# A gated linear unit in three passes of split operands, two gate tiles interleaved by halves of x, and the own-key part of attention on GpSimd

## The chip, the cores and the metric

The kernel runs on one core of a Trainium2 chip. The metric is the device time of one execution in microseconds (us), as the median of several runs.

## What is computed

One decoder layer over 1024 tokens of width 1024, in float32. The input is normalised and projected; half of the channels go through a diagonal state-space branch (S5), half through attention with a sliding window of 128 keys; both are gated, projected out, normalised, added to the input, and a gated embedding is added. What matters here, cut from the reference:

```python
# state-space branch: y is the output of the scan, 512 channels
g = jax.nn.gelu(y)
out = g * jax.nn.sigmoid(g @ w_glu + b_glu)          # the gated linear unit
ssm_out = out * jax.nn.silu(z_ssm)                   # z_ssm: 512 columns of the projection
# attention: each block of 128 queries sees the previous and its own block of keys
e = jnp.exp(scores - m)
probs = e / (jnp.sum(e, axis=-1, keepdims=True) + jnp.exp(sink - m))
out = jnp.einsum('bnkgqs,bnskd->bnqkgd', probs, vb)
mixed = jnp.concatenate([ssm_out, attn_out], axis=-1) @ w_out
```

## The kernel before

Everything lies transposed: channels on the 128 partitions, tokens along the free axis. A tensor of 512 channels has four tiles of 128 x 1024; a product with 1024 input channels runs over eight k-tiles of 128. TensorE accumulates in PSUM banks of 128 x 512, so a 1024-token result takes a pair of banks, one for each half of the tokens.

Most products are made with split operands. A float32 tile t is split into hi (a copy rounded to the type F32R, by ScalarE) and lo (t minus hi, by VectorE; `split_to`, L95). `products` (L119) then runs three F32R matmuls for each k-tile and half: weights hi times activations hi, weights hi times activations lo, weights lo times activations hi (L126, L128, L130). `load_split` (L108) loads weights through a staging tile w_st (two buffers) and splits them into w_hi and w_lo (four buffers each, of 128 x 4 x 128). The gated linear unit is the exception: there, y and w_glu are plain float32 and each k-tile takes one float32 matmul (L929).

After the state-space scan and most of the projection, a stage begins in which attention and other work share TensorE. The order of TensorE's work is written out by hand there. The other work is cut into "pieces", numbered n, which a table (`pieces`, filled by `at(n, f)`, L857) maps to functions. A time step t runs the attention steps that are due and then, except in every eighth step, the next piece. The order on the other engines is planned from the order of the program and priorities; attention steps have a higher priority (`AHEAD`).

The pieces, in their order:

- SsmGate (L866): the last two tiles (m = 2 and 3) of the state-space gate z. Each tile is a product over the eight k-tiles of x, one k-tile a piece: tile 2 has pieces 0 to 7, tile 3 has 8 to 15. Then come three steps: two scalings on VectorE out of PSUM, a tanh on ScalarE, and a product on VectorE, whose result goes to DRAM (z_dr). x lies in four big tiles: hi and lo of the first four k-tiles, hi and lo of the last four.
- `load_y` (L945), at piece 12: the output y of the scan comes back from DRAM (y_dr) in eight loads of 256 KB into a big tile y_all.
- Glu (L903): for each half hf of the tokens and each tile m, two pieces (16 to 31 in all), with two float32 matmuls each (L929). Three pieces before the first of them w_glu[m] is loaded (eight loads in all), one piece before it the gate's half tile z. Behind them come a tanh on ScalarE out of PSUM, two VectorE operations ((th + 1) y, and that times z / 2; L936, L937) and a split into m_hi and m_lo.
- OutHalf (L964): the product of m_hi and m_lo with the upper half of w_out, from piece 32 on; the first tile reads the tiles m = 0 to 2 at pieces 32 to 34 and m = 3 at piece 38.

Attention goes in 16 units, two to a block of 128 queries (even units: half 0, PSUM bank "w"; odd units: half 1, bank "y"). The steps of a unit: scores (TensorE; on GpSimd a copy of the sinks, L781), maxima (VectorE, out of PSUM, L796 and L804), exponents (ScalarE, L811), normalised (VectorE in even units, ScalarE in odd ones, L821 and L819), transposed (four TensorE transposes into a bank, then a ScalarE copy of it to a tile p, L826 and L828), parted (L830), values (L837) and gated (VectorE, L849). The 128 keys of the window lie in one row of 128, where a key of the previous block and one of the own block share a column. So values takes p times the previous block's v, plus the own-key part of p (p_own) times the difference of the two blocks' v (v_step). p_own is p times a triangular mask of ones (own_t), made by VectorE out of the same PSUM bank that ScalarE copies (L834). The values step of an even unit and the following odd unit come at the same time step: six steps after the transposes of the even one, two after those of the odd one.

Big tiles (128 x 4096 values, tag t16) have seven buffers. GpSimd also issues the query DMAs (L760, L761), four to a block.

Of the kernel before, what the change touches and what calls it, by code (L numbers as in the profile page):

```python
# [20 lines left out]
P = 128  # L21
D = 1024
T = 1024
KT = D // P
# [29 lines left out]
def layer_kernel(  # L54
# [6 lines left out]
    with ExitStack() as top:  # L61
# [685 lines left out]
        own_t = flat[:, 160:288]  # L747
        Q.memset(own_t, 1.0)
        Q.affine_select(out=own_t, in_=own_t, compare_op=ALU.is_ge, fill=0.0, base=0, pattern=[[1, P]], channel_multiplier=-1)

# [16 lines left out]
        class Unit:  # L767
# [62 lines left out]
            def parted(self):  # L830

                if self.b:
                    self.own = t2([P, 4, P], F32, "p_own", "qt")
                    V.tensor_tensor(out=self.own, in0=self.pt.rearrange("p (m q) -> p m q", m=4),  # L834
                                    in1=own_t.unsqueeze(1).broadcast_to([P, 4, P]), op=ALU.mult)
# [30 lines left out]
        class SsmGate:  # L866


            def __init__(self, m, n):
                self.m = m  # L870
                at(n - 3, self.load)
                for k in range(KT):
                    at(n + k, self.multiply, k)
                for i, f in enumerate((self.scale, self.tanh, self.store)):
                    at(n + KT + i, f)
# [27 lines left out]
        class Glu:  # L903


            def __init__(self, hf, m, n):
                self.hf, self.m = hf, m
                at(n - 3, self.load)
                at(n - 1, self.load_gates)
                for k in range(2):  # L910
                    at(n + k, self.multiply, k)
# [3 lines left out]
            def load(self):  # L915
                self.w = t2([P, 4, P], F32, "w_glu", "w_hi")
                with behind((self.hf, self.m) > (0, 1) and glu_in["last"]):
                    nc.sync.dma_start(out=self.w, in_=w_glu[self.m])

            def load_gates(self):  # L920
                self.zt = t4([P, 2, HALF], F32, "z_th")
                with behind(glu_in["last"]):
                    nc.sync.dma_start(out=self.zt[:, 0].rearrange("p (i c) -> p i c", i=HC), in_=z_dr[self.m][:, HC * self.hf : HC * self.hf + HC, :])

            def multiply(self, n):
                if n == 0:
                    self.ps = bank("mm")
                for k in (2 * n, 2 * n + 1):
                    PE.matmul(self.ps, lhsT=self.w[:, k, :], rhs=glu_in["y"][:, self.hf, k, :], start=k == 0, stop=k == 3)  # L929
# [4 lines left out]
            def gate(self):  # L934
                z, th = self.zt[:, 0], self.zt[:, 1]
                V.scalar_tensor_tensor(out=th, in0=th, scalar=1.0, in1=glu_in["y"][:, self.hf, self.m, :], op0=ALU.add, op1=ALU.mult)  # L936
                V.scalar_tensor_tensor(out=th, in0=th, scalar=0.5, in1=z, op0=ALU.mult, op1=ALU.mult)  # L937
# [5 lines left out]
        glu_in, glu_out = {}, []  # L943

        def load_y():  # L945
            y = glu_in["y"] = t16([P, 2, 4, HALF], F32, "y_all")
# [266 lines left out]
```

## Time and profile before

| | |
|---|---|
| median of 3 runs | 509.57 us (509.54 to 511.63) |
| the profiled execution | 510.56 us, its span 508.9 us |
| TensorE busy | 500.0 us, 98% of the span |
| VectorE busy | 372.6 us, 73% |
| ScalarE busy | 212.3 us, 42% |
| GpSimd busy | 35.0 us, 7% |

PE is TensorE, PEld its weight loads, DVE VectorE, ACT ScalarE, POOL GpSimd and SPq the queue that issues most DMAs. An instruction is told as line, engine, operation, output <- inputs, shapes. Matmuls are pipelined and the durations in the profile overlap, so the cost of one in a row of equal ones is read from start to start; the same holds for VectorE. A float32 matmul stands in the trace as two records. In brackets stands how long the engine had been idle before an instruction and what ended that.

### The profile page before, as it was taken

To read this page: it belongs to the slowest core of one execution; us is meant where nothing else is said; L and a number is where in the kernel's file an instruction comes from. 1 tells how busy PE (TensorE), PEld (TensorE's weight loads), DVE (VectorE), ACT (ScalarE), POOL (GpSimd) and SP (SyncE) were. 2 spreads that over 40 slices of the span, in tenths; PEclk is the share of its full clock that TensorE was granted. 3 is DMA by queue.
4 is the path that set the end of the run, shared out by engine and by line. 5 is a ranking of instruction groups with operands and counts; after the bars stand their busy time and mean duration, and the time that the engine had idled before them with its cause. 6 is when DMAs were issued, how large, how long until landed. Compare 5 with 4: busy or idle time off the path is not lost.

```text
span 508.9 us, 7268 instructions
## 1 busy us (share of the span) xinstructions
PE 500.0 (98%) x2445; PEld 403.2 (79%) x2445; DVE 372.6 (73%) x873; ACT 212.3 (42%) x450; POOL 35.0 (7%) x71
## 2 busy tenths in 40 slices
PE   7999999999999999999999999999999999999996
PEld 5788888888888888887555777877888888888886
DVE  3869999999999998557888766535565589564332
ACT  5777031322122232357566665556533362232311
POOL 1000000000000005231201320000000000000000
PEclk9999999999999999999999999999999999999999
DMA  7981624445555444564944521010212334134112
GB/s 257 394 261 60 201 84 134 124 120 149 140 133 133 119 139 108 155 178 155 301 165 146 175 63 32 22 41 1 103 63 82 124 120 130 42 124 146 62 43 83
DMA packets 54389, 65.05 MB, mean 128 GB/s; under 512 B 18384, under 2 KB 33232, under 8 KB 54352
## 3 DMA queue, kind: packets, MB, share of 16 engines
q1 hardware_dynamic: 50960, 58.09, 36.4%
q0 software_dynamic: 1536, 4.20, 3.1%
q10 hardware_dynamic: 1856, 2.31, 1.9%
q8 instruction: 19, 0.31, 0.3%
q14 instruction: 18, 0.15, 0.1%
HBM read 44.12 MB, written 11.01 MB: 108 GB/s over the span
## 4 chain that ended last, share of the span: by engine, by line
PE 88%; DVE 7%; DMA 2%; ACT 1%; issue 1%; SPq 0%; ACTq 0%
PE ps_mm L126 20%; PE ps_mm L128 19%; PE ps_mm L130 19%; PE ps_mm L929 6%; PE ps_tab L126 4%; PE ps_tab L128 4%; PE ps_tab L130 4%; PE ps_w L844 2%; PE ps_tab L788 1%; PE ps_y L635 1%; PE ps_tab L787 1%; PE ps_y L637 1%; PE ps_tab L546 1%; PE ps_y L844 1%; DMA x_st<-in_xT 1%; PE ps_w L559 1%
## 5 line engine op out<-in xcount | busy, mean ns | idle before, releaser
L96 ACT ACTIVATE w_hi<-w_st 128x512 fp32r<-128x512 f32 (+1 forms) x63 | 39.1, 620 | 120.1 <-PE ps_mm L128 70.6
L126 PE MATMUL ps_mm<-x_hi,w_hi 128*128 128x512 f32 x272 | 87.2, 396 | 1.8 <-ACT x_hi L194 1.4
L128 PE MATMUL ps_mm<-x_lo,w_hi 128*128 128x512 f32 x272 | 86.3, 395 | 0.6 <-DVE x_lo L195 0.6
L130 PE MATMUL ps_mm<-x_hi,w_lo 128*128 128x512 f32 x272 | 86.3, 393 | 0.0
L97 DVE TENSOR_TENSOR w_lo<-w_st,w_hi 128x512 fp32r<-128x512 f32 (+1 forms) x63 | 42.4, 673 | 27.0 <-ACT w_hi L96 24.3
L126 PEld LDWEIGHTS ps_mm<-x_hi,w_hi 128*128 128x128 f32 x272 | 50.1, 188 | 12.2 <-ACT x_hi L194 1.8
L128 PEld LDWEIGHTS ps_mm<-x_lo,w_hi 128*128 128x128 f32 x272 | 50.5, 188 | 11.2 <-DVE x_lo L195 1.4
L130 PEld LDWEIGHTS ps_mm<-x_hi,w_lo 128*128 128x128 f32 x272 | 50.9, 188 | 10.4
L811 ACT ACTIVATE sc<-sc,mx 128x129 f32<-128x129 f32 x64 | 25.1, 393 | 21.8 <-DVE mx L804 21.8
L128 PE MATMUL ps_mm<-h_lo,w_hi 128*128 128x512 f32 (+1 forms) x96 | 30.8, 380 | 0.0
L126 PE MATMUL ps_mm<-h_hi,w_hi 128*128 128x512 f32 (+1 forms) x96 | 30.8, 380 | 0.0
L130 PE MATMUL ps_mm<-h_hi,w_lo 128*128 128x512 f32 (+1 forms) x96 | 30.7, 380 | 0.0
L929 PE MATMUL ps_mm<-y_all,w_glu 128*128 128x512 f32 x64 | 29.7, 597 | 0.0
L1110 DVE SCALAR_TENSOR_TENSOR o_t<-o_t,pls 128x512 f32<-128x512 f32 (+1 forms) x17 | 10.8, 658 | 19.5 <-ACT o_t L1109 19.5
L126 PE MATMUL ps_mm<-m_hi,w_hi 128*128 128x512 f32 x64 | 21.2, 412 | 0.0
L128 PEld LDWEIGHTS ps_mm<-h_lo,w_hi 128*128 128x128 f32 x96 | 18.1, 188 | 3.5
L130 PEld LDWEIGHTS ps_mm<-h_hi,w_lo 128*128 128x128 f32 x96 | 18.0, 188 | 3.5
L126 PEld LDWEIGHTS ps_mm<-h_hi,w_hi 128*128 128x128 f32 x96 | 18.0, 188 | 3.4
L929 PEld LDWEIGHTS ps_mm<-y_all,w_glu 128*128 128x128 f32 x64 | 11.3, 189 | 11.3 <-issue 10.4
L128 PE MATMUL ps_mm<-m_lo,w_hi 128*128 128x512 f32 x64 | 19.9, 392 | 0.0
L130 PE MATMUL ps_mm<-m_hi,w_lo 128*128 128x512 f32 x64 | 19.9, 392 | 0.0
L781 POOL COPY sc<-sink 128x4 f32<-128x4 f32 x16 | 13.7, 855 | 75.4 <-PE ps_y L826 44.8
(279 smaller groups left out, 1021.6 us busy)
## 6 DMA issues: line engine op xcount, KB each, us to landing
w_st<-in_w_in SPq DMA_DIRECT2D x30, 256.0 KB
w_st<-in_w_out SPq DMA_DIRECT2D x16, 256.0 KB
w_st<-in_w_gate SPq DMA_DIRECT2D x16, 256.0 KB
x<-in_xS SPq DMA_DIRECT2D x8, 512.0 KB
out_T<-o_t SPq DMA_DIRECT2D x15, 256.0 KB
x_sq<-in_xT SPq DMA_DIRECT2D x4, 512.0 KB
x_st<-in_x SPq DMA_DIRECT2D x4, 512.0 KB
x_sq<-in_x SPq DMA_DIRECT2D x4, 512.0 KB
```

Of the source, the lines that this page charges most:

```text
L96: S.activation(hi, t, AF.Copy)
L97: V.tensor_tensor(out=lo, in0=t, in1=hi.bitcast(F32), op=ALU.subtract)
L126: yield PE.matmul(o, lhsT=wh, rhs=ah(ka, h), start=f, stop=False)
L128: yield PE.matmul(o, lhsT=wh, rhs=al(ka, h), start=False, stop=False)
L130: yield PE.matmul(o, lhsT=wl, rhs=ah(ka, h), start=False, stop=l)
L546: PE.matmul(ps[:, j, 0 : PC + P], lhsT=mt[:, g * P : (g + 1) * P], rhs=flat[:, 288 * j + 16 * odd : 288 * j + 16 * odd + PC + P], start=Tr ...
L559: PE.matmul(ps[:, g * NC : (g + 1) * NC], lhsT=m[:, g * P : (g + 1) * P], rhs=U[:, g, :], start=True, stop=True)
L781: Q.tensor_copy(out=self.sc.rearrange("p (a b) s -> p a b s", a=2)[:, :, :, P], in_=sink.rearrange("p (a b) -> p a b", a=2)[:, :, self.ms])
L811: S.activation(self.sc[:, m, :], self.sc[:, m, :], AF.Exp, bias=self.mx[:, m : m + 1], scale=-1.0, accum_out=self.sm[:, m : m + 1])
L844: PE.matmul(pv[64 * kv : 64 * kv + 64], lhsT=v[:, cols], rhs=p[:, 2 * kv : 2 * kv + 2, :], start=n == 0, stop=n == len(parts) - 1)
L929: PE.matmul(self.ps, lhsT=self.w[:, k, :], rhs=glu_in["y"][:, self.hf, k, :], start=k == 0, stop=k == 3)
L1110: V.scalar_tensor_tensor(out=t, in0=t, scalar=1.0, in1=pls[2 * m + h][:, a : a + n], op0=ALU.add, op1=ALU.mult)
```

## The change

Four things. The two gate tiles are interleaved: pieces 0 to 3 are tile 2 over the first four k-tiles of x, 4 to 7 tile 3 over the same, 8 to 11 tile 2 over the last four, 12 to 15 tile 3. y is loaded at piece 8, first half of the tokens first, and split into y_hi (ScalarE) and the low part in place (VectorE), tile by tile, at pieces 11 to 14 (first half) and 16 to 22 (second half). The gated linear unit runs `product` on split operands; w_glu is loaded and split once for both halves, its low part made by GpSimd. The gate loads both z and y by half tiles, and a VectorE operation z y / 2 (`weigh`) stands before the tanh, one operation behind it. The own-key part is selected on GpSimd from the copy p in SBUF.

```diff
-        own_t = flat[:, 160:288]
-        Q.memset(own_t, 1.0)
-        Q.affine_select(out=own_t, in_=own_t, compare_op=ALU.is_ge, fill=0.0, base=0, pattern=[[1, P]], channel_multiplier=-1)
...
                 if self.b:
                     self.own = t2([P, 4, P], F32, "p_own", "qt")
-                    V.tensor_tensor(out=self.own, in0=self.pt.rearrange("p (m q) -> p m q", m=4),
-                                    in1=own_t.unsqueeze(1).broadcast_to([P, 4, P]), op=ALU.mult)
+
+                    Q.affine_select(out=self.own, in_=self.p, compare_op=ALU.is_ge, fill=0.0, base=0,
+                                    pattern=[[0, 4], [1, P]], channel_multiplier=-1)
...
-            def __init__(self, m, n):
+            def __init__(self, m, ns):
                 self.m = m
-                at(n - 3, self.load)
-                for k in range(KT):
-                    at(n + k, self.multiply, k)
+                at(ns[0] - 3, self.load)
+                for k, n in enumerate(ns):
+                    at(n, self.multiply, k)
                 for i, f in enumerate((self.scale, self.tanh, self.store)):
-                    at(n + KT + i, f)
+                    at(ns[-1] + 1 + i, f)
...
-                at(n - 3, self.load)
+                if hf == 0:
+                    at(n - 3, self.load)
                 at(n - 1, self.load_gates)
+                at(n + 1, self.weigh)
...
             def load(self):
-                self.w = t2([P, 4, P], F32, "w_glu", "w_hi")
-                with behind((self.hf, self.m) > (0, 1) and glu_in["last"]):
-                    nc.sync.dma_start(out=self.w, in_=w_glu[self.m])
+                hi, lo = t2([P, 4, P], F32R, "g_hi", "w_hi"), t2([P, 4, P], F32R, "g_lo", "w_lo")
+                st = t2([P, 4, P], F32, "w_st", "w_st")
+                with behind(self.m > 1 and glu_in["last"]):
+                    nc.sync.dma_start(out=st, in_=w_glu[self.m])
+                S.activation(hi, st, AF.Copy)
+                Q.tensor_tensor(out=lo, in0=st, in1=hi.bitcast(F32), op=ALU.subtract)
+                glu_w.append([(hi, lo)])
...
-                    nc.sync.dma_start(out=self.zt[:, 0].rearrange("p (i c) -> p i c", i=HC), in_=z_dr[self.m][:, HC * self.hf : HC * self.hf + HC, :])
+                    for i, t in enumerate((z_dr, y_dr)):
+                        nc.sync.dma_start(out=self.zt[:, i].rearrange("p (i c) -> p i c", i=HC), in_=t[self.m][:, HC * self.hf : HC * self.hf + HC, :])
+
+            def weigh(self):
+                V.scalar_tensor_tensor(out=self.zt[:, 0], in0=self.zt[:, 0], scalar=0.5, in1=self.zt[:, 1], op0=ALU.mult, op1=ALU.mult)
...
-                for k in (2 * n, 2 * n + 1):
-                    PE.matmul(self.ps, lhsT=self.w[:, k, :], rhs=glu_in["y"][:, self.hf, k, :], start=k == 0, stop=k == 3)
+                y = tuple(lambda k, _, t=glu_in[n]: t[:, self.hf, k, :] for n in ("hi", "y"))
+                product([self.ps], glu_w[self.m], y, [(k, k) for k in (2 * n, 2 * n + 1)], first=n == 0, last=n == 1)
...
             def gate(self):
-                z, th = self.zt[:, 0], self.zt[:, 1]
-                V.scalar_tensor_tensor(out=th, in0=th, scalar=1.0, in1=glu_in["y"][:, self.hf, self.m, :], op0=ALU.add, op1=ALU.mult)
-                V.scalar_tensor_tensor(out=th, in0=th, scalar=0.5, in1=z, op0=ALU.mult, op1=ALU.mult)
+                V.scalar_tensor_tensor(out=self.zt[:, 1], in0=self.zt[:, 1], scalar=1.0, in1=self.zt[:, 0], op0=ALU.add, op1=ALU.mult)
...
         def load_y():
-            y = glu_in["y"] = t16([P, 2, 4, HALF], F32, "y_all")
-            for c, hf in [(c, hf) for c in range(4) for hf in range(2)]:
-                with behind(swaps[-1]):
-                    glu_in["last"] = nc.sync.dma_start(out=y[:, hf, c, :].rearrange("p (i c) -> p i c", i=HC), in_=y_dr[c][:, HC * hf : HC * hf + HC, :])
+            y = glu_in["y"] = t16([P, 2, 4, HALF], F32R, "y_all")
+            glu_in["hi"] = t16([P, 2, 4, HALF], F32R, "y_hi")
+            for hf in range(2):
+                for c in range(4):
+                    with behind(swaps[-1]):
+                        glu_in["last"] = nc.sync.dma_start(out=y[:, hf, c, :].bitcast(F32).rearrange("p (i c) -> p i c", i=HC), in_=y_dr[c][:, HC * hf : HC * hf + HC, :])
+
+        def split_y(hf, c):
+
+            t, hi = (glu_in[n][:, hf, c, :] for n in ("y", "hi"))
+            S.activation(hi, t.bitcast(F32), AF.Copy)
+            V.tensor_tensor(out=t, in0=t.bitcast(F32), in1=hi.bitcast(F32), op=ALU.subtract)
...
-            SsmGate(m, n)
-            n += KT
-        at(n - 4, load_y)
+            SsmGate(m, [n, n + 1, n + 2, n + 3, n + 8, n + 9, n + 10, n + 11])
+            n += 4
+        at(n, load_y)
+        n += 8
...
             for m in range(4):
+                at(n - 5 - m if hf == 0 else n - 8, split_y, hf, m)
                 Glu(hf, m, n)
                 n += 2
```

## Rows read from the trace of the kernel before

**Rows 1.** From the page: busy time, share of the span and instructions of each engine; TensorE's granted clock in 40 slices, in tenths of full speed; the chain of work that ended last, by engine.

```profile
PE 500.0 (98%) x2445; PEld 403.2 (79%) x2445; DVE 372.6 (73%) x873; ACT 212.3 (42%) x450; POOL 35.0 (7%) x71
...
PEclk9999999999999999999999999999999999999999
...
PE 88%; DVE 7%; DMA 2%; ACT 1%; issue 1%; SPq 0%; ACTq 0%
```

**Rows 2.** Busy time by stretch: the stretch from:to, its length, busy us (x instructions) of PE, PEld, DVE, ACT and POOL, granted clock, DMA share, GB/s.

```profile
245.00:282.75 37.75, 37.75 (x149) 19.65 (x148) 32.72 (x96) 24.91 (x72) 6.67 (x12) 1.00 0.61 199
282.75:343.00 60.25, 60.25 (x337) 47.61 (x337) 35.60 (x122) 35.07 (x107) 7.41 (x13) 1.00 0.21 61
```

**Rows 3.** TensorE in order of time: start, us, engine, line, operation, output <- inputs, count of equal ones merged.

```profile
229.61 0.63 PE L126 MATMUL ps_mm<-x_hi,w_hi 128*128 128x512 f32 x2
...
245.00 3.85 PE L929 MATMUL ps_mm<-y_all,w_glu 128*128 128x512 f32 x8
248.69 0.60 PE L826 MATMUL ps_y<-sides,sc 128*128 128x128 f32 x4
...
260.40 5.31 PE L929 MATMUL ps_mm<-y_all,w_glu 128*128 128x512 f32 x12
265.55 0.60 PE L826 MATMUL ps_y<-sides,sc 128*128 128x128 f32 x4
...
282.40 0.60 PE L826 MATMUL ps_y<-sides,sc 128*128 128x128 f32 x4
...
288.53 0.73 PE L126 MATMUL ps_mm<-m_hi,w_hi 128*128 128x512 f32 x2
```

**Rows 4.** DMA around the loads of y: by stretch, as in rows 2 (four rows); the DMA queue of SP in order of time (two rows); the weight load that waited for y (one row).

```profile
228.00:236.00 8.00, 8.00 (x41) 6.50 (x40) 6.54 (x23) 6.39 (x23) 0.19 (x1) 1.00 0.16 60
236.00:245.00 9.00, 9.00 (x54) 7.08 (x53) 5.97 (x28) 4.14 (x18) 2.27 (x5) 1.00 0.92 261
245.00:255.00 10.00, 10.00 (x43) 5.07 (x43) 9.56 (x28) 6.64 (x20) 3.50 (x5) 1.00 0.95 310
255.00:265.00 10.00, 10.00 (x37) 5.14 (x34) 7.99 (x26) 6.68 (x20) 0.66 (x1) 1.00 0.43 145
...
235.63 4.53 SPq L949 DMA_DIRECT2D y_all<-y_dr  x8
...
250.60 3.94 SPq L923 DMA_DIRECT2D z_th<-z_dr  x3
...
247.72 0.30 PEld L929 LDWEIGHTS ps_mm<-y_all,w_glu 128*128 128x128 f32 x2 [0.82 <-DMA y_all<-y_dr]
```

**Rows 5.** TensorE in the last gate tile at the end of the kernel, whose first half runs on one bank: the first of the 24 matmuls of 128x512 and the one behind the last.

```profile
493.06 0.39 PE L126 MATMUL ps_mm<-h_hi,w_hi 128*128 128x512 f32 x1
...
498.50 0.28 PE L126 MATMUL ps_mm<-h_hi,w_hi 128*128 128x256 f32 x1
```

**Rows 6.** Groups of instructions by line from 228 to 283.7 us: count, busy us, mean ns of one, idle time before them.

```profile
L889 DVE SCALAR_TENSOR_TENSOR z_half<-ps_mm,preb 128x512 f32<-128x512 f32 x4 | 4.1, 1070 | 3.6 <-PE ps_mm L130 3.6
L899 DVE SCALAR_TENSOR_TENSOR z_tanh<-z_tanh,z_half 128x1024 f32<-128x1024 f32 x2 | 2.4, 1220 | 0.0
...
L96 ACT ACTIVATE w_hi<-w_st 128x512 fp32r<-128x512 f32 x4 | 2.5, 620 | 0.0
```

**Rows 7.** ScalarE and VectorE in order of time: the normalisation of an odd unit, and the low part of the gated tile m = 2 of the second half.

```profile
273.41 1.28 ACT L819 ACTIVATE sc<-sc,sm 128x128 f32<-128x128 f32 x4 [0.49 <-DVE sm L816]
...
282.95 0.68 DVE L97 TENSOR_TENSOR m_lo<-z_th,m_hi 128x512 fp32r<-128x512 f32 x1
```

**Rows 8.** VectorE in order of time, in the runs beside which GpSimd had work.

```profile
193.27 0.68 DVE L339 TENSOR_TENSOR s<-s,co 128x512 f32<-128x512 f32 x1
...
198.63 0.68 DVE L339 TENSOR_TENSOR w<-w,sw 128x512 f32<-128x512 f32 x1
...
220.24 1.76 DVE L97 TENSOR_TENSOR bq_lo<-q_f,bq_hi 128x512 fp32r<-128x512 f32 x2
...
283.56 0.68 DVE L936 SCALAR_TENSOR_TENSOR z_th<-z_th,y_all 128x512 f32<-128x512 f32 x1
...
285.36 0.68 DVE L834 TENSOR_TENSOR p_own<-ps_y,sides 128x512 f32<-128x512 f32 x1
```

**Rows 9.** The own-key products: their durations in ns (min/median/max, the seven of the even units), and the row of the list of waits (us in total, times, longest).

```profile
L834 DVE TENSOR_TENSOR p_own<-ps_w,sides x7: 684/691/692, 242.1 to 336.4; 128x512 f32<-128x512 f32 x7
...
DVE p_own L834 <- ACT p L828: 12.3, 8, 2.2
```

**Rows 10.** GpSimd in order of time.

```profile
194.10 5.26 POOL L781 COPY sc<-sink 128x4 f32<-128x4 f32 x1 [7.39 <-DVE s L339]
...
219.67 1.15 POOL L798 TENSOR_SCALAR_AFFINE_SELECT sc<-sc 128x512 f32<-128x512 f32 x1 [2.74 <-ACT sc L790]
...
226.21 0.65 POOL L798 TENSOR_SCALAR_AFFINE_SELECT sc<-sc 128x512 f32<-128x512 f32 x1
227.57 0.19 POOL L781 COPY sc<-sink 128x4 f32<-128x4 f32 x1 [0.71 <-PE ps_w L826]
...
283.13 2.36 POOL L781 COPY sc<-sink 128x4 f32<-128x4 f32 x1 [7.96 <-PE ps_y L826]
```

**Rows 11.** An odd unit: ScalarE's copy of the transposes, and the product with its own-key part on TensorE.

```profile
249.47 0.58 ACT L828 COPY p<-ps_y 128x512 f32<-128x512 f32 x1
...
254.94 0.60 PE L844 MATMUL ps_y<-p_own,v_step 128*64 128x256 f32 x4
```

More of the change, by code (lines that the diff above doesn't have):

```diff
@@ L941, in split @@
                 split_to(glu_out[0][:, self.m, hs], glu_out[1][:, self.m, hs], self.zt[:, 1])
-        glu_in, glu_out = {}, []
+        glu_in, glu_out, glu_w = {}, [], []
         def load_y():
-            y = glu_in["y"] = t16([P, 2, 4, HALF], F32, "y_all")
-            for c, hf in [(c, hf) for c in range(4) for hf in range(2)]:
-                with behind(swaps[-1]):
-                    glu_in["last"] = nc.sync.dma_start(out=y[:, hf, c, :].rearrange("p (i c) -> p i c", i=HC), in_=y_dr[c][:, HC * hf : HC * hf + HC, :])
+            y = glu_in["y"] = t16([P, 2, 4, HALF], F32R, "y_all")
[8 more added lines that the diff above has]
+            V.tensor_tensor(out=t, in0=t.bitcast(F32), in1=hi.bitcast(F32), op=ALU.subtract)
         n = 0
         for m in range(2, 4):
-            SsmGate(m, n)
-            n += KT
-        at(n - 4, load_y)
+            SsmGate(m, [n, n + 1, n + 2, n + 3, n + 8, n + 9, n + 10, n + 11])
+            n += 4
+        at(n, load_y)
+        n += 8
         for hf in range(2):
```

## The prediction

> **What bounds the kernel now.** I read the page's busy times and its chain of waits first. TensorE is busy for 500.0 of 508.9 us, carries 88% of the chain, and its granted clock is full in all 40 slices, that is 2.4 GHz [rows 1]. Next the busy time by stretch: in the stretch of the gated linear unit (245 to 282.75 us) TensorE is busy all the time, while VectorE has 32.72 of 37.75 us and ScalarE 24.91; behind it TensorE is as full [rows 2]. So a cut on TensorE is worth its full length, as long as VectorE, ScalarE, GpSimd and the DMAs deliver on time; I read the timelines for how much time they have left.
>
> I call "piece" the unit of the hand-written order: six products of split operands, or two plain f32 ones.
>
> **Part 1, the products.** Each f32 matmul of the gated linear unit stands in the trace as two records; 12 of them take 260.40 to 265.55 us, 0.429 us a record [rows 3]. The 64 records cost 27.5 us. The first eight take 3.69 us (245.00 to 248.69) where 3.43 is due, so 0.26 us of waiting for y lies there; the weight load of the last of them waited for y's DMA [rows 3, 4]. The change runs 32 x 3 = 96 matmuls of 128x512, each on one bank with its own weight load. Just that form is seen in the last gate tile: 24 of them in 5.44 us (493.06 to 498.50), 0.2267 us each [rows 5]. 96 of them are 21.8 us. TensorE saves 27.5 + 0.26 - 21.8 = 6.0 us; a piece falls from 1.72 to 1.36 us. The borders to transposes, scores and values are the same in number before and after; I let them cancel, within some 0.3 us either way. The last two gate tiles keep their 48 matmuls each; only the order of x's halves changes: 0.
>
> **Part 2, y comes earlier and is split.** Before, y is loaded when the first x tile is free, after piece 11; the eight loads are issued from 235.63 us on, and the seventh (the last of the first half) is awaited until 247.7 [rows 4]. The interleaved order frees both first-half x tiles after piece 7, at 229.6 us [rows 3], where the queues have little to do (a DMA share of 0.16 in 228 to 236, against 0.92 in 236 to 245) [rows 4]. At the 261 GB/s of that second stretch the first half of y (1 MB) takes 4 us, and is there at about 235. Its four splits are four ScalarE copies (0.62 us [rows 6]) and four VectorE subtractions (0.60 us from start to start [rows 7, 8]): some 3 us when alone, against 10 us until piece 16. On SP's queue the eight issues (4.5 us [rows 4]) now stand ahead of the store of tile 2's z, which goes four pieces back itself and is read from piece 20 on. I cost all this at nothing; it would cost what comes after 245.0.
>
> The gates now load y again (8 x 256 KB more), and w_glu is loaded four times instead of eight (4 x 256 KB less). The queue moved 199 GB/s in this stretch and up to 310 in a part of it [rows 2, 4]. 199 x 37.75 = 7.5 MB, and 1 MB more in 31.8 us is 268 GB/s: below 310, at nothing.
>
> **Part 3, VectorE and ScalarE in 31.8 us instead of 37.75.** VectorE had 32.72 us of work. Four own-key products leave (4 x 0.60), four splits of y's second half come (4 x 0.60), the gate keeps two operations a tile: still 32.7. What is carried in: tile 2 of the gate now ends at piece 11 instead of 7, so its two scalings (1.07 us each) and its 1.22 us product [rows 6] come four pieces later, after 235.9; up to 2 us of this lands behind 245. Three low parts of later weights (1.8 us) may slip out behind it. So about 33 us of VectorE work stand against 31.8 us, before GpSimd's share (part 4, up to 2 us more): it ends 1 to 3 us late. What covers this is lead. A normalised row is ready at 274.69 us and transposed at 282.40; the low part of the third tile of the second half is ready at 283.55 and read at 288.53 [rows 3, 7]. Leads of 7.7 and 5.0 us; the first shrinks with the four pieces in it by 1.4 to 6.3. After that VectorE has 35.6 us of work in 60.25 [rows 2] and catches up. So nothing on the path; if the cover were gone, the 1 to 3 us would be paid in full. ScalarE's 24.9 us grow by four splits of y and some two of weights (6 x 0.62) to 28.6 of 31.8: also covered.
>
> The tanh of a tile now overwrites what the new product z x y / 2 has read, so it stands on ScalarE's queue behind that VectorE operation and behind two loads; exponents are queued behind it. The tightest is tile 3 of the first half, whose z is written only now: its load is among three issued by 254.5 us, and seven y loads took 12.1 us, 1.7 each [rows 4], so z and y are there by 257.9. Its products end before at 260.40 + 8 x 0.429 = 263.8 [rows 3], after eight pieces of 0.36 us less and the 0.26 at 260.7. Margin 2.8 us.
>
> **Part 4, own keys on GpSimd.** Fourteen VectorE products of 0.69 us go, and with them the 12.3 us in which VectorE stood waiting for ScalarE's copy [rows 9]. Fourteen selections come on GpSimd. The same operation on the same shape ran twice: 0.65 us with VectorE idle, 1.15 us beside VectorE [rows 10]. What a busy VectorE does to GpSimd is seen in the sink copies: 0.19 us alone, but 2.36 us from 283.13, until 0.13 us after VectorE's first operation with a PSUM input (285.36) behind a run with two SBUF inputs; and 5.26 us beside a run of such operations from 193.27 to 199.31 us [rows 7, 8, 10]. So a selection takes 0.65 us plus up to 2.4 us, in the worst row 5 us. And it takes from VectorE too: two low parts took 1.76 instead of 1.28 us beside the 1.15 us selection [rows 8], 0.5 us each, 2 us for four in this stretch (none to 2; I take 2, the only row).
> The Trainium skill says that GpSimd's SBUF interfaces are shared with VectorE, in contention with instructions that have two SBUF inputs (GPSIMD Engine Reference, Key points); by that rule, these rows agree.
>
> How much time is there? ScalarE's copy of an odd unit ends at 250.05 us, and the product with its own-key part starts at 254.94 [rows 11]: 4.9 us, 4.2 with two shorter pieces, for a selection of 0.65 to 3.05 us. It is hidden, except behind a run of 3.5 us or more. Even units have six steps between instead of two. Queued behind a selection are the sink copies and the four query DMAs of a block, whose queries are read seven steps later: at nothing. The transposes' bank now waits for the copy alone: no loss.
>
> The low parts of w_glu are four two-input subtractions on GpSimd, which no row shows: between 0.65 us (the one-input selection) and 2.3 us (twice the slow one); I take 1.2. They are needed 3 pieces after the load, and the unguarded first two long after: at nothing on the path.
> The Trainium skill says that two-input elementwise work is about twice as slow on GpSimd as on VectorE and belongs on VectorE (GPSIMD Engine Reference, Engine selection); by that rule it would be an estimated 1.4 us each, and no row here shows it.
>
> The four w_glu tiles hold all four hi and lo buffers until pieces 25 to 31, so w_out comes later: its first tile gets a buffer after piece 25 and is needed at 32 (over 9 us for 1.3 us of splitting), the second after 27 for 35. At nothing.
>
> **Sum.** -6.0 us, and 0.3 us for small late arrivals: -5.7. The profiled execution took 510.56 us (span 508.9), so 504.9 for it; it lay 1.0 us above the median, and from the median 509.57 it is **503.9 us**.
>
> **Rivals.**
> *A, VectorE becomes the bound of the stretch.* For it: 33 us of work in 31.8, 35 with GpSimd's share, and in-order waits between VectorE and ScalarE that a full queue can't hide. Against: leads of 5.0 and 6.3 us. If the 1 to 3 us are paid: 505 to 507.
> *B, the own-key part comes late.* A selection caught in a run of 5 us takes 5.65 us, 1.5 more than it has. Seven odd units: up to 10 us, but runs that long are seen only in the scan stage before. Two to four units late: 3 to 6 us back, 507 to 510.
> *C, slower: the tanh holds ScalarE's queue.* It decides once z and y arrive so late that the wait eats ScalarE's 3.8 idle us and the 6.3 us of lead, 10 us in all or 1.3 us a tile; behind that each us is a us of TensorE. To lose the 6 us and 3 more, the eight tiles wait 2.4 us each: 513 us. A tile needs 512 KB in 4.0 us, 130 GB/s; the lowest stretch of the unit moved 145 [rows 4], with less asked. So little speaks for it.
>
> **Chances.** What a measurement can tell from no change is 0.5%, 2.5 us. Forecast, TensorE's own saving, 502.3 to 505.3: 0.60. A: 0.20, three quarters of it below 507.0. B: 0.10, mostly within 507 to 510. C: 0.10. Faster by over 0.5%: 0.60 + 0.15 = 0.75; within: 0.05 of A, 0.09 of B and 0.01 of C, 0.15; slower: 0.10. The range reaches into B: 502.3 to 508.8 leaves out half of B, C and a little at the lower end.
>
> **What would show it.** In the profile after, 96 products under the three-pass lines at 0.227 us from start to start between about 245 and 277; TensorE's waits in that stretch under 0.5 us. A shows as waits of TensorE for VectorE or ScalarE on the transposes or on the first w_out products; B as waits of the value products for GpSimd; C as ScalarE waiting at the tanh for the gate product. If y's loads start later than 231 us, part 2 is wrong. If VectorE's idle time there vanishes and TensorE still keeps its pace, the leads were the right cover.

## The result and the profile after

The changed kernel takes 518.30 us (median of 4 runs, 516.68 to 519.95), the kernel before, run beside it, 510.39: a ratio of 1.0147, 95% interval 1.0124 to 1.0171. The forecast was 503.9 and its range ended at 508.8. The profiled execution took 516.68 us (span 515.0, so 1.6 under the median; differences below are between the two profiles). From the page, as in [rows 1]:

```profile
PE 498.7 (97%) x2477; PEld 412.0 (80%) x2477; DVE 371.9 (72%) x867; ACT 218.5 (42%) x462; POOL 48.6 (9%) x87
...
PEclk9899999999999999999998999999999999999998
...
PE 86%; DMA 6%; DVE 5%; issue 1%; ACT 1%; SPq 0%; DVEq 0%
```

TensorE works 1.3 us less in a span 6.1 us longer: it stands idle. DMA, 2% of the chain of waits before, is 6%. Some slices no longer have the full clock. TensorE in order of time, as in [rows 3] (in brackets: idle time before, and what ended it):

```profile
244.45 0.66 PE L822 MATMUL ps_w<-sides,sc 128*128 128x128 f32 x4 [2.54 <-DVE q_f L846]
...
259.70 0.66 PE L822 MATMUL ps_w<-sides,sc 128*128 128x128 f32 x4 [0.52 <-DVE q_f L846]
...
270.44 0.36 PE L783 MATMUL ps_tab<-kk,bq 128*128 128x256 f32 x1 [1.33 <-DVE mx L800]
...
271.22 0.40 PE L128 MATMUL ps_mm<-y_all,g_hi 128*128 128x512 f32 x1
271.45 0.39 PE L130 MATMUL ps_mm<-y_hi,g_lo 128*128 128x512 f32 x1
...
272.94 0.60 PE L841 MATMUL ps_w<-p_own,v_step 128*64 128x256 f32 x4
...
275.84 0.40 PE L130 MATMUL ps_mm<-y_hi,g_lo 128*128 128x512 f32 x1
279.52 0.66 PE L822 MATMUL ps_w<-sides,sc 128*128 128x128 f32 x4 [3.28 <-DVE q_f L846]
279.93 0.63 PE L126 MATMUL ps_mm<-y_hi,g_hi 128*128 128x512 f32 x1
280.36 0.63 PE L128 MATMUL ps_mm<-y_all,g_hi 128*128 128x512 f32 x1
...
288.01 0.60 PE L822 MATMUL ps_y<-sides,sc 128*128 128x128 f32 x4
```

The products have the pace of the forecast (271.22 to 271.45: 0.23 us). But three times TensorE stops (stands idle) at the transposes of an even unit (L822, before L826) until q_f, VectorE's gated product (L846, before L849), has run, and once at the scores of a unit (L783) for the maxima: 7.67 us in all. Behind the longest stop the matmuls stand 0.43 us apart instead of 0.227, until 283.35: some 1.6 us more. From the first scores of the stage (216.80 before, 217.84 after) to the odd transposes ahead of the w_out products (282.40 [rows 3], and 288.01) it takes 70.17 us instead of 65.60: 4.6 more, where 6.0 less was forecast. Another 1.0 us is lost ahead of the stage (216.80 against 217.84), where the granted clock was 0.93 in 0 to 25 us; of the thirteen experiments below that contain the whole or most of the change ten have 1.00 there and three 0.93, so it comes and goes, and I don't count it to the change. The last 0.5 us of the 6.1 lie behind the stage.

Why the transposes wait for q_f: an even unit's values (L841) go into bank "w", which has one buffer. The next even unit's transposes go into the same bank, two steps later, and q_f must have read the values first. In the rows above the last values of the bank start at 272.94; the odd unit's values and one piece of six products (the last at 275.84) are all that stands between. VectorE meanwhile, ahead of the first and the third stop:

```profile
239.38 0.69 DVE L962 TENSOR_TENSOR y_all<-y_all,y_hi 128x512 fp32r<-128x512 f32 x1
239.97 0.88 DVE L817 TENSOR_SCALAR sc<-sc,sm 128x128 f32<-128x128 f32 x4
...
241.09 1.30 DVE L962 TENSOR_TENSOR y_all<-y_all,y_hi 128x512 fp32r<-128x512 f32 x2
...
242.83 1.22 DVE L962 TENSOR_TENSOR y_all<-y_all,y_hi 128x512 fp32r<-128x512 f32 x1
243.98 0.41 DVE L846 TENSOR_TENSOR q_f<-ps_w,z_att 128x256 f32<-128x256 f32 x1
...
274.28 0.69 DVE L930 SCALAR_TENSOR_TENSOR z_th<-z_th 128x512 f32<-128x512 f32 x1 [0.83 <-DMA z_th<-y_dr]
...
278.44 0.69 DVE L930 SCALAR_TENSOR_TENSOR z_th<-z_th 128x512 f32<-128x512 f32 x1 [0.52 <-DMA z_th<-y_dr]
279.05 0.42 DVE L846 TENSOR_TENSOR q_f<-ps_w,z_att 128x256 f32<-128x256 f32 x1
```

VectorE runs its instructions in the order of its queue: in these rows q_f starts only when those ahead of it are done, also one that waits. At the first stop q_f (243.98) stands behind the splits of y (L962), those of the second half too (three of the four, from 241.09 on), which nobody needs before piece 24. At the third it stands behind `weigh` (L930), which waits for the second load of y. The busy time in stretches, as in [rows 2, 4], and two rows of VectorE's list of waits in 210 to 300 us (us in total, times, longest):

```profile
236.00:245.00 9.00, 6.46 (x37) 4.41 (x36) 8.55 (x21) 7.65 (x20) 4.31 (x5) 1.00 0.77 247
245.00:255.00 10.00, 10.00 (x55) 8.57 (x55) 9.36 (x24) 6.82 (x22) 3.69 (x6) 1.00 0.48 171
...
275.00:283.00 8.00, 4.72 (x19) 3.57 (x18) 6.15 (x19) 5.55 (x17) 1.84 (x4) 0.82 0.77 221
```
```profile
DVE z_th L930 <- DMA z_th<-y_dr: 3.4, 4, 1.2
...
DVE z_th L930 <- DMA z_th<-z_dr: 1.6, 1, 1.6
```

VectorE is nearly full in 236 to 245 (8.55 of 9 us; before, 5.97 [rows 4]). In 275 to 283 it has 6.15 of 8, but most of that idle time lies behind q_f, where VectorE waits for TensorE (281.67 to 283.59); ahead of q_f, from 275.00 to 279.05, it has 3.54 of 4.05. What made q_f late here is the sum of VectorE's waits for loads since 259.6: the two rows above, 5.0 us. The chain of waits leads from that stop back through them (start, us, what):

```profile
252.44 1.24 DVE z_tanh L896
...
253.70 3.29 DMA z_dr<-z_tanh
...
257.06 5.69 DMA z_th<-z_dr
...
263.48 0.69 DVE z_th L930
264.17 1.05 DVE m_lo L97
...
265.24 0.32 SPq L927
...
265.60 3.36 DMA z_th<-y_dr
...
269.05 0.69 DVE z_th L930
...
272.85 0.61 DVE m_lo L97
...
273.48 0.32 SPq L927
...
273.84 4.51 DMA z_th<-y_dr
...
278.44 0.69 DVE z_th L930
279.13 0.35 DVE q_f L846
```

The chain is a loop. A tile z_th is free for the next load when its low part (m_lo, L97, on VectorE) is made. Twice the load is issued (L927, 265.24 and 273.48) some 0.02 us behind the end of an m_lo, and takes 3.36 and 4.51 us; `weigh` waits for it and holds back what stands behind it, q_f among it. So late work on VectorE makes the loads late, and late loads make VectorE late.

### The profile page after: what moved, and what is told of

Its sections match the earlier page's. It is cut to its first block, busy times and chain, and to the rows that moved or that the text cites. A ratio compares the mean times of both kernels' runs of the same rounds, so it can differ in the third digit from the quotient of the medians.

```text
span 515.0 us, 7375 instructions
## 1 busy us (share of the span) xinstructions
PE 498.7 (97%) x2477; PEld 412.0 (80%) x2477; DVE 371.9 (72%) x867; ACT 218.5 (42%) x462; POOL 48.6 (9%) x87
## 4 chain that ended last, share of the span: by engine, by line
PE 86%; DMA 6%; DVE 5%; issue 1%; ACT 1%; SPq 0%; DVEq 0%
PE ps_mm L126 21%; PE ps_mm L128 21%; PE ps_mm L130 21%; PE ps_tab L126 4%; PE ps_tab L128 4%; PE ps_tab L130 4%; DMA z_th<-y_dr 2%; PE ps_tab L546 2%; PE ps_y L635 1%; PE ps_w L559 1%; PE ps_y L637 1%; DMA x_st<-in_xT 1%; DMA z_th<-z_dr 1%; DMA y_all<-y_dr 1%; PE ps_w L841 1%
## 5 line engine op out<-in xcount | busy, mean ns | idle before, releaser
L97 DVE TENSOR_TENSOR w_lo<-w_st,w_hi 128x512 fp32r<-128x512 f32 (+1 forms) x63 | 42.4, 674 | 35.3 <-ACT w_hi L96 27.0
L792 DVE COPY_PREDICATED ps_tab<-sides,ps_tab 128x256 f32<-128x256 int32 x28 | 11.8, 427 | 13.8 <-PE ps_tab L784 13.4
L783 PE MATMUL ps_tab<-kk,bq 128*128 128x256 f32 (+1 forms) x64 | 16.3, 286 | 1.3 <-DVE mx L800 1.3
L1125 ACT ACTIVATE o_t<-ps_mm,hb_gate 128x512 f32<-128x512 f32 (+1 forms) x12 | 7.7, 665 | 23.0 <-PE ps_mm L130 15.9
```

The costliest lines, as they stand in the source:

```text
L97: V.tensor_tensor(out=lo, in0=t, in1=hi.bitcast(F32), op=ALU.subtract)
L783: PE.matmul(o, lhsT=l, rhs=kk_hi[:, kv, k0 : k0 + wk], start=True, stop=False)
L792: V.copy_predicated(out=ps[:, :, 0:P], mask=own.unsqueeze(1).broadcast_to([P, 2, P]), data=ps[:, :, P : 2 * P])
L1125: S.activation(t, o, AF.Tanh, bias=hb_gate[:, m : m + 1], scale=0.5)
```

## The experiments

Four theories of what makes the kernel slower. **Q**: the order of VectorE's queue puts q_f behind work that could wait. **D**: the second loads come late (z is stored four pieces later; z_th shares four buffers with z's tiles). **G**: GpSimd and VectorE slow each other. **F**: VectorE has too much work in any order. "Stage" is the length measured above, in the profiled execution: 65.60 us before, 70.17 after. Each kernel is the changed one with the edit shown, unless said otherwise.

**Own-key part back on VectorE** (the lines removed in the diff restored).

> The changed kernel with the own-key part of the exponents back on VectorE (out of PSUM, times the mask, as before); all else as changed. Theory Q (VectorE's queue is in order; its gated product, which frees the bank that the next transposes need, stands late behind splits of y and behind products that wait for loads): no gain, VectorE gets 14 x 0.6 us back, so the ratio to the kernel before stays at 1.010 to 1.025 and TensorE still waits some 6 us or more for the gated product. Rival G (GpSimd's selections and VectorE slow each other on SBUF): at least 2 us less, ratio under 1.010, and the long VectorE operations of the changed kernel (1.2 to 1.65 us for 0.7 to 0.9) get short.

513.92 us, ratio 1.0070 (1.0055 to 1.0085); stage 67.36. G's number, and Q's was missed: with q_f late, what the selections on GpSimd cost VectorE counts, about half of the loss. But three stops at the even transposes stayed (2.24 and 0.98 us for q_f, 0.64 for a normalisation), so it isn't the whole cause.

**Gate from y's high part**: no `weigh`, no second load; y's low part is left out of the gate.

```diff
-                at(n + 1, self.weigh)
...
-                    for i, t in enumerate((z_dr, y_dr)):
-                        nc.sync.dma_start(out=self.zt[:, i].rearrange("p (i c) -> p i c", i=HC), in_=t[self.m][:, HC * self.hf : HC * self.hf + HC, :])
+                    nc.sync.dma_start(out=self.zt[:, 0].rearrange("p (i c) -> p i c", i=HC), in_=z_dr[self.m][:, HC * self.hf : HC * self.hf + HC, :])
...
-                V.scalar_tensor_tensor(out=self.zt[:, 1], in0=self.zt[:, 1], scalar=1.0, in1=self.zt[:, 0], op0=ALU.add, op1=ALU.mult)
+                z, th = self.zt[:, 0], self.zt[:, 1]
+                V.scalar_tensor_tensor(out=th, in0=th, scalar=1.0, in1=glu_in["hi"][:, self.hf, self.m, :].bitcast(F32), op0=ALU.add, op1=ALU.mult)
+                V.scalar_tensor_tensor(out=th, in0=th, scalar=0.5, in1=z, op0=ALU.mult, op1=ALU.mult)
```

> The changed kernel without the product z x y / 2 ahead of the tanh and without the second load of y; the gate takes y's hi part in its place (its low part is left out of the gate alone), with two VectorE operations behind the tanh as before. Theory Q: the waits of VectorE for z_th's loads go (5 us in the changed kernel) and with them the last two stalls of TensorE (1.5 and 3.4 us) and the half clock behind the second (1.6 us): 6 us less, ratio 1.000 to 1.007; the first stall, 2.7 us at 242, stays. Rival G: less than 2 us change. Rival D (the late thing is the DMA queues, not the place of the product in VectorE's queue): half of it, ratio about 1.008.

509.02 us, 0.9967 (0.9951 to 0.9982); stage 63.29. Better than Q's 1.000 to 1.007. All stops for q_f are gone but the first (2.25 us at 243.53).

**Splits of y's second half held** behind the last gated product written ahead of each (two splits behind the first block's, two behind the second's).

```diff
-                V.tensor_tensor(out=q_f[:, self.ms, self.qs], in0=self.pv, in1=z_att[:, self.ms, self.qs], op=ALU.mult)
+                glu_in["gated"] = V.tensor_tensor(out=q_f[:, self.ms, self.qs], in0=self.pv, in1=z_att[:, self.ms, self.qs], op=ALU.mult)
...
-            S.activation(hi, t.bitcast(F32), AF.Copy)
-            V.tensor_tensor(out=t, in0=t.bitcast(F32), in1=hi.bitcast(F32), op=ALU.subtract)
+            with behind(hf and glu_in["gated"]):
+                S.activation(hi, t.bitcast(F32), AF.Copy)
+                V.tensor_tensor(out=t, in0=t.bitcast(F32), in1=hi.bitcast(F32), op=ALU.subtract)
```

> The changed kernel with the four splits of y's second half held behind the first block's gated product on ScalarE and VectorE (in the changed kernel they stand ahead of it). Theory Q: the first stall of TensorE, 2.7 us at 242, goes; the others stay or grow a little, as 2.4 us of VectorE work move into the gated linear unit: 1 to 3 us less, ratio 1.008 to 1.013. Rival F (VectorE is simply overfull): the 2.7 us come back later, ratio 1.013 to 1.018.

511.31 us, 1.0005 (0.9985 to 1.0025); stage 64.70. Better than Q said, and not F's number: the order of four splits is worth 1.4% of the kernel. The first stop is gone, although VectorE is busy for all of 236 to 245 us here (9.00 us, 8.55 above): there it was the order and not the amount of work. The three later stops take 3.60 us instead of 5.13 (0.97, 0.81 and 1.82, where 0.52, 1.33 and 3.28 were), with no low clock.

**Own-key part alone**, put into the kernel before.

> The kernel before with only the own-key part moved to GpSimd (products in f32, gate tiles in their old order). Theory Q (what makes the changed kernel late is other work standing ahead of the gated product in VectorE's queue: splits of y, and products that wait for their loads): VectorE has slack there, so no change, ratio 0.997 to 1.003. Rival G (GpSimd's selections slow VectorE's operations with two SBUF inputs, or come late themselves; taking them out of the changed kernel gave back 0.8%): 1 to 4 us slower, ratio 1.002 to 1.008, with TensorE waiting for p_own or for the gated product.

510.24 us, 1.0005 (0.9989 to 1.0020). No effect by itself.

**Even transposes one step later**.

```diff
-        steps = ((Unit.gated, 14, 10), (Unit.values, 13, 9), (Unit.transposed, 7, 7), (Unit.parted, 7, 7), (Unit.normalized, 5, 5),
+        steps = ((Unit.gated, 14, 10), (Unit.values, 13, 9), (Unit.transposed, 8, 7), (Unit.parted, 8, 7), (Unit.normalized, 5, 5),
```

> The changed kernel with the transposes (and the own-key part) of even units one time step later, so that one piece more (1.36 us) lies between the values of a block and the next transposes into the same bank. Theory Q: each stall on the gated product shrinks by up to 1.4 us (2.7, 0.7 and 3.4 us): 3 to 4 us less, and less of the half clock: ratio 1.004 to 1.009. Rival F: VectorE stays the bound and the stalls turn up at other instructions, ratio above 1.012.

512.50 us, 1.0046 (1.0031 to 1.0061), as Q said. TensorE's waits for q_f fall to 0.2 us, but a stop of 3.52 us appears at 237.84, at the odd transposes, for ScalarE's normalisation. On ScalarE's queue the early splits of y stand ahead of it, and two of them had waited for their load (0.46 and 0.99 us).

**Weighing late** (`weigh` two pieces later, the tanh left in PSUM).

> The changed kernel with the product z x y / 2 two steps later, next to the second gate operation; the tanh is written back into its PSUM bank, so that it needs not wait for that product. Same loads, same arithmetic, splits of y where they were. Theory Q: the waits of VectorE for z_th's loads, now 3.4 us for y and 1.6 for z, fall under 1.5 us and the last two stalls of TensorE (1.5 and 3.4 us with the half clock behind it) go, as without the second load: ratio 0.996 to 1.004. Rival D (the loads themselves are too late, by the four buffers and the queues, wherever the product stands): the waits stay at the later place, ratio 1.006 to 1.014.

518.21 us, 1.0164 (1.0145 to 1.0183): Q was wrong, and it is above D's 1.014 too. VectorE's wait for the load of y even grows to 5.6 us, in five places, and the longest stop to 4.92 us: there q_f (279.22) again stands right behind a `weigh` (278.61) that waited 2.12 us for its load. So the place of the weighing doesn't cure it as long as the load is this late. This spoke for D.

**Held splits and gate from y's high part.**

> Both repairs of VectorE's queue in one: the splits of y's second half held behind the first gated product, and the gate from y's hi part without a second load (its low part is left out of the gate alone). Theory Q: both groups of stalls go at once and TensorE's saving of 5.7 to 6.0 us shows, ratio 0.988 to 0.991. Rival F (VectorE is overfull in the stretch, whatever the order): the held splits push others late, ratio 0.994 to 0.999.

506.37 us, 0.9940 (0.9921 to 0.9960); stage 61.05, 4.55 us below before. Q's number was missed, F's lower bound just reached. One stop of 1.03 us is left. With the two parts of the cause away, three quarters of the 6.0 us are there in the stage of the profile, and about half in the ratio (0.6% is 3.1 us). VectorE is busy for 31.19 us of the 32 from 245 to 277: what is left can be F's, and no run tells.

**Held splits and late weighing.**

> The splits held and the product z x y / 2 late, with the tanh in PSUM: the whole computation, nothing left out. Theory Q: like the run with the gate from the hi part, perhaps 1 us behind it for eight more loads: ratio 0.988 to 0.993. Rival D: the eight loads of y keep it behind, ratio 0.996 to 1.002. Rival F: 0.994 to 0.999.

510.98 us, 1.0003 (0.9985 to 1.0022): D's number, and that of the held splits alone. VectorE still waits 4.5 us for y's second loads.

**Interleaving alone**, in the kernel before, with y loaded at piece 8.

> The kernel before with one part of the change: the two gate tiles interleaved by halves of x and the loads of y sent eight pieces earlier; products of the unit in whole f32, own key on VectorE, no second load of y. Theory Q (VectorE's in-order queue: the gated product is late behind splits and weighing that this kernel doesn't have): TensorE loses nothing in bank w and wins at most the wait for y at the start of the unit, 0.996 to 1.001 of before. Theory D (the interleaving holds tile 2's z and tile 3's z in the four large buffers at once, and the loads of z come late for that): the gate of the first tiles waits for z, 1.003 to 1.010.

511.38 us, 1.0009 (0.9997 to 1.0021); stage 65.37. No gain and no loss: neither the order of the two tiles nor the early loads cost anything by themselves.

**y summed on GpSimd**: held splits; y = hi + lo instead of the second load (the splits and the load as above, cut here).

```diff
...
+                hi, lo = (glu_in[n][:, self.hf, self.m, :].bitcast(F32) for n in ("hi", "y"))
+                Q.tensor_tensor(out=self.zt[:, 1], in0=hi, in1=lo, op=ALU.add)
...
```

> The changed kernel, whole computation, with two edits: the splits of y's second half stand behind the first gated product of the unit before, and y for the gate isn't loaded again but summed on GpSimd from its high and low parts (eight additions of 512 elements, each 1.3 to 2.2 us of GpSimd by the rows of the w_glu low parts). Theory D (the second load of y is what VectorE's queue waits for): as in the run with hi alone, 0.993 to 0.998 of before. Theory G (GpSimd beside VectorE is the price): the additions lengthen VectorE's instructions by some 0.5 us each, 4 us in all, of which half reaches TensorE, 0.999 to 1.005. Theory F (VectorE is full whatever its order): about 1.000.

517.21 us, 1.0144 (1.0128 to 1.0159): all theories wrong, G by direction least. The first stop is back (2.39 us at 244.33), although the splits are held. Two rows of GpSimd and two of VectorE ahead of it:

```profile
239.86 1.29 POOL L928 TENSOR_TENSOR z_th<-y_hi,y_all 128x512 f32<-128x512 f32 x1
241.11 1.28 POOL L920 TENSOR_TENSOR g_lo<-w_st,g_hi 128x512 fp32r<-128x512 f32 x1
```
```profile
239.72 3.35 DVE L817 TENSOR_SCALAR sc<-sc,sm 128x128 f32<-128x128 f32 x4
242.99 0.42 DVE L792 COPY_PREDICATED ps_tab<-sides,ps_tab 128x256 f32<-128x256 int32 x1
```

Four normalisations that take 0.88 us in the profile after (239.97) take 3.35, one of them 2.76, while GpSimd runs two instructions with two inputs, an addition and a subtraction: VectorE hardly gets on until they end at 242.39. It hits the queue ahead of q_f.

**Both cures, own-key part on VectorE** (held splits, gate from y's high part).

> The run with both cures (splits of y's second half held, gate from y's high part alone, so y's low part is left out of the gate and there is no weighing and no second load) with the own-key part of the exponents back on VectorE as one product. Theory G: GpSimd's selections cost more beside VectorE than they take off it, 0.988 to 0.993 of before, below the 0.994 of that run. Theory F: VectorE gets some 0.7 us more for each of the seven units in the stage, up to 5 us, of which what finds no gap reaches TensorE, 0.997 to 1.002. Theory Q: the queue has room once nothing waits at its head, 0.992 to 0.997.

507.03 us, 0.9935 (0.9923 to 0.9947), against 0.9940 with it on GpSimd: the same. Q's number: what the selections cost in the first experiment counts only as long as q_f is late.

**Another bank for the values** of units 2 and 4, and nothing else.

```diff
-                pv = self.pv = bank("wy"[self.half], (P, 2, P))
+                pv = self.pv = bank("mm" if self.half == 0 and self.b in (1, 2) else "wy"[self.half], (P, 2, P))
```

> The changed kernel with nothing else changed than the bank of two units' values: the even units 2 and 4 write their values into one of the four banks of the unit's products, so the next transposes in bank w need not wait for their gated product. Loads, splits, weighing and GpSimd stay as they are. Theory Q with its bank (the one piece between the values and the next transposes in bank w is what makes the late queue a loss): the stalls of 0.5 and 3.3 us behind q_f and the half clock behind the longer one go, the first stall of 2.5 us stays, 1.003 to 1.008 of before. Theory D (the late loads hold the gated product back from everything): the wait comes back elsewhere, as a wait for the maxima or for the unit's tanh, 1.011 to 1.017. Theory F: half of it comes back, 1.008 to 1.011.

513.35 us, 1.0060 (1.0040 to 1.0081); stage 64.72. Q's number: the two later stops for q_f and the low clock are gone, though VectorE waits 4.4 us for y's loads, more than the 3.4 in the profile after. The first stop stayed (2.24 us), as it had to: there the unit's four banks belong to the interleaved gate tiles. This shows that at these two units the bank is what turns a late q_f into lost time.

**Held splits and the other bank**, whole computation.

> The changed kernel, whole computation, with the two cures of bank w that each worked alone: the splits of y's second half behind the first gated product, and the values of the even units 2 and 4 in one of the unit's banks. Theory Q with its bank: the two cures take different stalls (2.5 us at the first one, 0.5 and 3.3 us and the half clock at the later two), so their gains add up: after's 1.0147 less 0.014 less 0.009 gives 0.991 to 0.997 of before. Theory D (what is left of the forecast's gain is held by the late loads of z and y): the waits for the maxima of 1 to 2 us grow, 0.997 to 1.001.

510.24 us, 0.9984 (0.9966 to 1.0002); stage 63.82. The cures don't add up; D is nearer. TensorE waits no more for q_f. What is left, on VectorE and then on TensorE:

```profile
258.73 0.69 DVE L930 SCALAR_TENSOR_TENSOR z_th<-z_th 128x512 f32<-128x512 f32 x1 [2.27 <-DMA z_th<-y_dr]
```
```profile
266.37 0.36 PE L783 MATMUL ps_tab<-kk,bq 128*128 128x256 f32 x1 [1.95 <-DVE mx L800]
```

The loop again: the late load holds VectorE's queue for 2.27 us, the m_lo behind it (260.38) frees a buffer late, the next load (from 261.45, 3.42 us) is waited for by the `weigh` at 265.00, and the maxima stand behind that. TensorE stops 1.95 us, with a mean clock of 0.83 in the ten us around (265 to 275).

**The same and the weighing late.**

> The same two cures and the weighing two pieces later, behind the tanh's matmuls, the tanh left in PSUM; whole computation. Theory Q with its bank: without the bank the late weighing gave nothing, because q_f was late behind other things too; now the gated product has time, and the weighing no longer waits at the head of the queue, 0.990 to 0.995 of before. Theory D: the loads come no earlier for it and the gate ends as late, the same as the run with the two cures to within 0.002.

510.55 us, 0.9989 (0.9971 to 1.0007): the same, as D said.

**The same two cures, w_glu's low parts on VectorE** (`V.tensor_tensor` for `Q.tensor_tensor` in Glu's load).

> The same two cures, and the four low parts of w_glu made on VectorE (0.68 us each by the splits of y) instead of GpSimd (1.3 to 2.2 us each); the own-key part stays on GpSimd. Theory G (GpSimd's instructions with two operands stretch what VectorE does beside them): VectorE gains more than the 2.7 us that it takes over, 0.002 to 0.005 below the run with the two cures. Theories Q and F: 2.7 us more in a queue that is over nine tenths busy, 0.001 to 0.005 above it.

508.82 us, 0.9952 (0.9934 to 0.9970): 0.0032 below the run with GpSimd's low parts, within G's bounds; the intervals overlap by 0.0004. The whole computation, and faster than both kernels. Its profiled execution was the slowest of its eight (510.51 us), with a stop of 2.23 us at 235.48 for ScalarE's normalisation, again behind splits of y that waited for their load (1.63 and 1.04 us), so its stage (64.99) doesn't stand for the median.

## Why the prediction was wrong, point by point

- **Part 1, the products**: right. 0.227 us each; with the stops gone (held splits, gate from hi) the stage of the profile is 4.55 us shorter, 5.6 with the one stop left taken off.
- **Part 2, the early loads**: right in itself; y's first splits ran from 232.2 us, the wait for y is gone, and the interleaving alone changes nothing. What I passed over is what comes with it: the splits of the second half were ready so early that they were queued before 245 us, ahead of q_f. "Its four splits are ... some 3 us" counted the first half alone; VectorE's 236 to 245 us went from 5.97 to 8.55 us busy. On ScalarE the early splits can hold up a normalisation, as in two of the experiments.
- **Part 3, "What covers this is lead"**: this step failed. I forecast VectorE 1 to 3 us late, and took as cover the 7.7 us of a normalised row and the 5.0 us of the w_out operand. The shortest lead on VectorE's queue was another: q_f, which must run between the values and the next transposes in the same bank. The trace of before could have told (TensorE's rows of bank w, and VectorE's of q_f):

```profile
240.86 0.60 PE L826 MATMUL ps_w<-sides,sc 128*128 128x128 f32 x4
...
254.08 0.60 PE L844 MATMUL ps_w<-p_own,v_step 128*64 128x256 f32 x4
...
257.30 0.60 PE L826 MATMUL ps_w<-sides,sc 128*128 128x128 f32 x4
```
```profile
239.12 0.42 DVE L849 TENSOR_TENSOR q_f<-ps_w,z_att 128x256 f32<-128x256 f32 x1
...
255.07 0.42 DVE L849 TENSOR_TENSOR q_f<-ps_w,z_att 128x256 f32<-128x256 f32 x1
```

  q_f ended 1.8 us ahead of need (255.49 to 257.30), and at the first block 1.3 us (239.54 to 240.86). The shorter piece takes 0.36 us off the 1.8. An operation with less than 1.5 us to spare can't stand behind 1 to 3 us of lateness. The term "0.3 us for small late arrivals" in the sum came to 7.67 us of stops and 1.6 us of low clock. Giving the values another bank (1.0147 to 1.0060) and taking four splits from ahead of q_f (to 1.0005) each removed a part of the loss.
- **Part 3, "Margin 2.8 us"** for tile 3's z and y: used up. The load of z_th took 5.69 us for tile 3's z, behind a store of 3.29, and up to 4.51 for the y of later tiles; I had taken 1.7 us a load from a queue in full stream, and had not asked when the buffers come free. And the wait fell not on ScalarE's tanh but on `weigh`, at the head of VectorE's queue, ahead of q_f and the maxima.
- **Part 4**: the own-key part is hidden from TensorE, as forecast (alone 1.0005; no matmul stops for it in the profile after). It was not free beside a late q_f, though: back on VectorE it gave 0.0077 of the ratio (1.0147 to 1.0070). "I take 1.2" for w_glu's low parts: 1.37, 1.29, 1.30, and 2.24 us beside VectorE. They were not free either: beside the one of 2.24 us, from 241.27 on, a split of y ahead of q_f took 1.22 us instead of 0.69 (242.83 and 239.38 above), and on VectorE, with the cures, the kernel gains 0.0032.

The Trainium skill's rule (GPSIMD Engine Reference, Engine selection), by which I gave an estimated 1.4 us, agrees with three of these four rows. The Trainium skill's rule on shared SBUF interfaces (GPSIMD Engine Reference, Key points) I had set against VectorE's instructions with two SBUF inputs. The row of 3.35 us is of instructions with one tensor input in SBUF; the Trainium skill names there, as its other case, VectorE instructions in a two-port mode. Whether these four run in it, no row here shows.

- **Rivals**: A named the engine and its sign (TensorE waiting at the transposes), and had 505 to 507, because it charged only VectorE's lateness and not what a stop adds: the low clock and the next stops. B did not happen in the profile after (in two experiments TensorE waited for p_own, 0.9 and 1.1 us). C had a load at the head of an in-order queue and a price on the right side (513), but on ScalarE and with 0.10. What took place is A and C together, by the bank.

How the loss divides between the queue's order, the loads and GpSimd is settled only roughly, as the cures overlap: held splits 1.4% of the kernel, gate from hi 1.8%, both 2.1%; the own-key part back on VectorE 0.8%, and nothing once both are applied. The gate from hi takes away loads and waits at once, so it does not tell a late load from a slow one. The chain of waits shows late loads issued as soon as a buffer is free; why they then take 3.4 to 5.7 us was not separated, and no run had more buffers.

## What to carry to other kernels

For an engine with an in-order queue, forecast how late it ends, but compare that with the shortest lead among all that stands in its queue, read from each pair of write and reuse; here a PSUM bank with one buffer gave the shortest. Work that becomes ready earlier also runs earlier, ahead of what is due: when loads move forward, hold back what isn't needed yet. An operation that waits for a load should not be written ahead of what another engine waits for, and a time saved on the bounding engine shortens every lead that is counted in its pieces.

## What the runs showed of the hardware

The granted clock was 0.82 of full on average in 275 to 283 us. It was still 1.00 in 279.5 to 280.0, after TensorE had idled for 3.28 us, and 0.50, the lower level (1.2 GHz), in 280.5 to 283.4. It stayed full behind an idle of 2.54 us (1.00 in 236 to 245 and in 245 to 255 us above) and yet fell in another run behind one of 1.95 us (held splits and the other bank: 1.00 in 266 to 267, 0.50 in 268 to 270), so the length of the idle alone doesn't decide. GpSimd's two-input instruction on 128x512 takes 1.28 to 1.37 us in these rows, and VectorE's instructions with one tensor input stood almost still meanwhile: 3.35 instead of 0.88 us. Beside VectorE's splits it took 2.24 us itself.
